# Weight splits of a fused encoder block made 2048 columns at a time, with a raw ring of two tiles and PSUM banks evacuated in pairs

## The chip, the cores and the metric

The kernel runs on one core of a Trainium2 chip. The metric is the device time of one execution in microseconds, of which less is better. A core has TensorE (PE) for matrix products, VectorE (DVE), ScalarE (ACT) and GpSimd (POOL) for elementwise work, and SyncE (SP), whose queue issues most of the DMA transfers here. PE writes its products to PSUM, eight banks of 512 float32 columns per partition; everything else works on tiles in SBUF, 128 partitions high.

## The reference

One layer of an encoder block is computed on 256 tokens of width 2048, in float32:

```
hn   = rmsnorm(x);            proj = hn @ w_in                  # 2048 x 3616
mix  = [ssd_mixer(...), pool_mixer(...)] @ w_out                # 2048 x 2048
h    = x + rmsnorm(mix)
up   = rmsnorm(h) @ w_ffn_up                                    # 2048 x 11264
ff   = (gelu(conv3(gate)) * val) @ w_ffn_down                   # 5632 x 2048
h    = h + rmsnorm(ff)
gate = sigmoid(rmsnorm(h) @ w_ple_gate)                         # 2048 x 2048
out  = h + rmsnorm(gate * (p @ w_ple))
```

Nearly all of the work is the six weight matrices. Their 51 million float32 values, some 204 MB, are read from device memory in each execution.

## The kernel before, in words

**Precision and units.** A float32 product is made from rounded operands. Each weight is split into a high part (rounded) and a low part (what the rounding left), each activation too, and PE sums three products: high by high, high by low, low by high. The weights come in units of 128 x 2048 values, 1 MB, laid out so that one DMA brings one unit. `raw` (L157) takes a tile of the ring "raw" (three tiles of 2048 columns) and has SP load a unit into it. `split` (L142) takes a pair of tiles from the rings "whi" and "wlo" (five tiles each, of 1056 columns, so half a unit), has ACT round 1024 columns into the high part (L153) and DVE subtract it from the raw values into the low part (L154). PE reads only the parts. A raw tile can be loaded again when its last split is done; a tile of parts can be written again when PE has read it for the last time. Tiles of one ring are handed out in turn, and the framework puts the waits.

**Stages.** They follow each other on PE: a first projection (`dtu`, L454, units of 1056 columns of which half come into raw tiles and half into other pages), the convolved inputs (`feature_major`, L339), then `z`, the output projection `wo`, the up projection, the down projection `dn` and the gate projection `gt`. `z`, `wo`, `dn` and `gt` go through `token_major` (L305), which works in two halves of 1024 output columns and collects products in two pairs of PSUM banks.

**The up projection** (L1007 to L1032) is the longest stage: 176 pieces of 1024 weight columns, two to a unit, four to a block of 256 output columns. Its instructions on ACT, DVE and SP run in the order in which they are written (`in_order`, L199). Five pieces are split ahead; then for each piece PE's products are issued (`feature_pairs`, L355), after the fourth piece the block's two banks are evacuated (`total`, L367: per bank an ACT copy L370 of one half and a DVE addition L371 of the other), and the piece five further on is split (`next_part`, L961), with a new unit's load at every second piece. Blocks of gate and value columns alternate by two. Between them stand the convolution, the gelu and the product of both (`gate_conv`, `gelu`, `value_out`).

**Jobs in the up projection's shadow.** A list `jobs_at` hangs further work on pieces. Thirty-seven units of `w_down` and `w_gate` are fetched (SP, L120) into pages, their four column blocks summed by DVE (`add_blocks`, L249, four additions of 512 columns), and 35 of them stored to device memory again (POOL, L244). For thirteen pairs of activation tiles, sums are made (`pair_sums`, L784: four DVE operations of 128 columns, an ACT copy, a DVE subtraction) and stored.

**Fast units.** With these sums, a unit of `dn` or `gt` needs seven block products in place of eight (`seven_products`, L255): 21 matmuls of 512 columns, where a plain unit has 24. Such a unit loads 1536 columns of weights into a raw tile (L261) and the stored sums into a page `t` (L265), and splits four times: `a` (512 columns), `b` (1024), `d` and `c` (1024 each of the sums). `dn` has 32 fast units and 12 plain ones, `gt` five fast and eleven plain, `wo` three fast, whose sums are made in place in the raw tile between the splits. `combine` (L283) then joins the seven products in PSUM. Of the second half of `gt`, the last four units are first all split and then multiplied in one pass over the output columns (tail of 4 in L321), two of them into pages kept in `spare` (L1140).

**PSUM.** The pool "pmain" has six tiles of one bank, and `main` (L83) hands them out two at a time; "pmisc" has two more.

Of the kernel before, what the change touches and what calls it, by code (L numbers as in the profile page):

```python
# [17 lines left out]
P = 128  # L18
L = 256
# [34 lines left out]
def build(nc, a, out):  # L54
# [6 lines left out]
    with tile.TileContext(nc) as tc, \  # L61
# [6 lines left out]
            tc.tile_pool(name="pmain", bufs=6, space=bass.MemoryType.PSUM) as pm, \  # L68
# [14 lines left out]
        def main(name):  # L83
            return [pm.tile([P, 512], F32, tag="main", name=f"{name}_{i}") for i in range(2)]
# [14 lines left out]
        r0 = wp.tile([P, 2048], F32, tag="raw", bufs=3, name="dtur0")  # L99
# [42 lines left out]
        def split(name, src, nel, cuts=()):  # L142

            if name in ready:
                return ready.pop(name)
            if name in spare:
                hi, lo = spare.pop(name)
            else:
                hi = wp.tile([P, 1056], F32R, tag="whi", bufs=5, name=f"{name}h")
                lo = wp.tile([P, 1056], F32R, tag="wlo", bufs=5, name=f"{name}l")  # L150
            for c0, c1 in zip((0, *cuts), (*cuts, nel)):
                s = slice(c0, c1)
                last["act"] = ins(nc.scalar.copy(hi[:, s], src[:, s]))  # L153
                last["dve"] = ins(nc.vector.tensor_sub(lo[:, s], src[:, s], hi[:, s].bitcast(F32)))  # L154
# [94 lines left out]
        def add_blocks(r):  # L249

            v = r.rearrange("p (b c) -> p b c", b=4)
            for i, j in ((1, 0), (0, 3), (3, 1), (2, 3)):
                nc.vector.tensor_add(v[:, i], v[:, i], v[:, j])  # L253

        def seven_products(name, stage, w, k0, c0, a_, acc, alt, start, stop):  # L255
# [49 lines left out]
        def token_major(name, w, c0, ks, get, acc, tail=1, fast=(), alt=None, sums=None, at=()):  # L305
# [3 lines left out]
            for u in range(nu):  # L309
# [8 lines left out]
                r = None if f"{name}{k0}_0" in ready else raw(f"{name}r{k0}", w[c0 // 1024, k0 // 2])  # L318
                for j in range(2):
                    group.append((k0 + j, *split(f"{name}{k0}_{j}", r and r[:, j * 1024:(j + 1) * 1024], 1024)))  # L320
# [18 lines left out]
        def feature_major(name, w, get, acc):  # L339

            for u in range(4):
                r = raw(f"{name}r{u}", w[u])
                for j in range(2):
                    wh, wl = split(f"{name}{u}_{j}", r[:, j * 1024:(j + 1) * 1024], 1024)
                    for kk in range(2):
                        k = 4 * u + 2 * j + kk
                        xh, xl = get(k)
                        for f in range(4):
                            s = slice(kk * 512 + f * P, kk * 512 + (f + 1) * P)
                            for q, (ww, xx) in enumerate(((wh, xh), (wh, xl), (wl, xh))):  # L350
                                mm(acc[f // 2][:, f % 2 * L:(f % 2 + 1) * L], ww[:, s], xx,
                                   k == 0 and q == 0 and f % 2 == 0, k == NK - 1 and q == 2)
                aside()

        def feature_pairs(n, part, get, acc):  # L355
# [4 lines left out]
            for kk in range(4):  # L360
                k = 4 * n + kk
                for f in range(2):
                    s = slice(kk * 256 + f * P, kk * 256 + (f + 1) * P)
                    mm(acc[f], wh[:, s], get.both(k), k == 0, False)
                    mm(acc[f][:, L:], wl[:, s], get(k)[0], False, k == NK - 1)

        def total(o, acc):  # L367

            for f in range(2):
                nc.scalar.copy(o[:, f * L:(f + 1) * L], acc[f][:, L:])  # L370
                nc.vector.tensor_add(o[:, f * L:(f + 1) * L], o[:, f * L:(f + 1) * L], acc[f][:, :L])  # L371
# [82 lines left out]
        for u in range(0, NK, 2):  # L454
            r = [wp.tile([P, 2048], F32, tag="raw", bufs=3, name=f"dtur{u}") if u else r0, page(f"dtur{u + 1}")]
# [19 lines left out]
            for j in range(2):  # L475
                k = u + j
                with tc.issue_after(front[0]), tc.issue_after(front[1]):
                    wh, wl = split(f"dtu{k}", r[j][:, :1056], 1056, ((352, 704), (704,))[k] if k < 2 else ())
# [305 lines left out]
        def pair_sums(name, s, o, a11, a21, a12, a22):  # L784


            s1, s2, s3, s4 = (s[:, i * P:(i + 1) * P] for i in range(4))
            nc.vector.tensor_sub(s1, a22, a21)
            nc.vector.tensor_sub(s3, a11, a21)
# [6 lines left out]
        def sums_in(o):  # L796
            return {f"s{i + 1}": (o[:, i * P:(i + 1) * P], o[:, 512 + i * P:512 + (i + 1) * P]) for i in range(4)}

        class Sums:
# [5 lines left out]
            def __call__(self, k):  # L805
                if k not in self.got:
                    n = len(self.got)
                    if n % 2 == 0:
# [6 lines left out]
                                            *(v[:, i * P:(i + 1) * P] for i in range(4)))  # L815
# [119 lines left out]
        def hid_sums_of(k, s, o):  # L935
            return pair_sums(f"he{k}", s, o, *(hid_part(k)[:, i * P:(i + 1) * P] for i in range(4)))
# [24 lines left out]
        def next_part():  # L961

            n = len(parts)
            if n < NPIECES:
                s, v, i = blocks[n // 4]
                name = f"u{'gv'[v]}{s}{i}"
                if n % 2 == 0:
                    slab["raw"] = raw(f"{name}r{n // 2 % 2}", w_up[v, s, i, n // 2 % 2])
                parts.append(split(f"{name}{n // 2 % 2}_{n % 2}", slab["raw"][:, n % 2 * 1024:(n % 2 + 1) * 1024], 1024))
# [37 lines left out]
        with in_order():  # L1007
            for _ in range(5):
                next_part()
            for n in range(NPIECES):  # L1010
                s, v, i = blocks[n // 4]
                if n % 4 == 0:
                    acc = main(f"{'gv'[v]}a{s}{i}")
# [9 lines left out]
                next_part()  # L1023
# [38 lines left out]
        def ple_parts():  # L1062

            r = raw("ple1r0", w_ple[1, 0])
            for j in range(2):
# [176 lines left out]
```

## Time and profile before

| what | us |
|---|---|
| timed runs, median of 3 (lowest to highest) | 1116.89 (1116.58 to 1117.33) |
| profiled execution, first to last instruction (span) | 1115.6 |
| PE busy in it | 1104.8 (99%) |
| DVE busy | 957.5 (86%) |
| ACT busy | 721.7 (65%) |
| DMA traffic | 347.29 MB, 311 GB/s over the span |

The stages in the profiled execution, by the chain of work that ended last: first projection until 53 us, convolved inputs until 142, `z` until 198, `wo` until 287, up projection from 293 to 788, down projection until 1011, gate projection to the end. "ga" and "va" are the PSUM tiles of the up projection, "dna" and "dns" those of the down projection, "gt" and "gts" of the gate. Line L90 is the helper through which every matmul goes, L120 the one for SP's loads, L153 and L154 the two halves of a split. A row of instructions has line, engine, operation, output and inputs, shapes, count, then busy time and mean ns of one, then the idle time of its engine ahead of it and what ended it. A row of waits has who waited for whom, the total, the number of times and the longest. A row of DMA issues ends with the median us from issue to landing. The lines themselves stand in the prediction.

### The profile page before, as it was taken

How to read it: one execution, taken by the hardware profiler on the slowest of the kernel's cores; microseconds unless marked ns; L12 is line 12 of the kernel's file. 1: busy time of each engine (PE TensorE's matmuls, PEld its weight loads, DVE VectorE, ACT ScalarE, POOL GpSimd, SP SyncE). 2: the span in 40 equal slices, each digit the busy share in tenths (PEclk: the TensorE clock that was granted, in tenths of full speed). 3: DMA queues.
4: the chain of work that ended last, by engine and by line, in shares of the span. 5: the costliest groups of instructions: out<-in, count | busy, mean ns of one | idle time of the engine just before them, and what ended most of it. 6: DMA issues, size and time to landing. Idle time of an engine off the chain costs nothing.

```text
span 1115.6 us, 16022 instructions
## 1 busy us (share of the span) xinstructions
PE 1104.8 (99%) x5948; PEld 951.8 (85%) x5948; DVE 957.5 (86%) x1334; ACT 721.7 (65%) x1048; POOL 68.5 (6%) x140
## 2 busy tenths in 40 slices
PE   9999999999999999999999999999999999999997
PEld 9999988888888888888888888888888888877876
DVE  6478997799868898888888888888899999989895
ACT  6847662555775564665655645657589778867673
POOL 0200000100100000000000000000000000001001
PEclk9999999999999999999999999999999999999999
DMA  9752447454599999999899999999999899996763
GB/s 362 314 194 109 164 156 284 151 189 158 199 362 401 387 378 376 359 375 369 346 377 382 354 380 366 353 391 391 361 379 382 329 343 400 418 376 229 264 237 105
DMA packets 54943, 347.29 MB, mean 311 GB/s; under 512 B 6096, under 2 KB 6992, under 8 KB 20176
## 3 DMA queue, kind: packets, MB, share of 16 engines
q1 hardware_dynamic: 44064, 289.53, 67.3%
q0 software_dynamic: 10368, 56.10, 13.4%
q8 instruction: 47, 0.77, 0.3%
q10 hardware_dynamic: 432, 0.62, 0.2%
q14 instruction: 32, 0.26, 0.1%
HBM read 297.48 MB, written 48.76 MB: 310 GB/s over the span
## 4 chain that ended last, share of the span: by engine, by line
PE 94%; DVE 2%; ACT 1%; DMA 1%; issue 1%; POOL 0%; POOLq 0%; ACTq 0%; DVEq 0%
PE ga L90 22%; PE va L90 22%; PE dna L90 12%; PE woa L90 7%; PE xbc L90 5%; PE gt L90 5%; PE z L90 4%; PE dns L90 4%; PE dtu L90 4%; PE dn0s L90 2%; PE dn1s L90 2%; DMA dtur<-w_dtu 1%; PE pw L90 1%; PE yd L90 1%; PE gts L90 1%
## 5 line engine op out<-in xcount | busy, mean ns | idle before, releaser
L90 PE MATMUL ga<-wox,ug_0h 128*128 128x512 f32 x352 | 125.5, 395 | 0.0
L90 PE MATMUL ga<-wox,ug_1h 128*128 128x512 f32 x352 | 125.1, 394 | 0.0
L90 PE MATMUL va<-wox,uv_1h 128*128 128x512 f32 x352 | 124.8, 393 | 0.0
L90 PE MATMUL va<-wox,uv_0h 128*128 128x512 f32 x352 | 124.8, 393 | 0.0
L90 PE MATMUL ga<-wox,ug_1l 128*128 128x256 f32 x352 | 99.1, 282 | 0.0
L90 PE MATMUL va<-wox,uv_1l 128*128 128x256 f32 x352 | 99.1, 281 | 0.0
L90 PE MATMUL va<-wox,uv_0l 128*128 128x256 f32 x352 | 99.1, 281 | 0.0
L90 PE MATMUL ga<-wox,ug_0l 128*128 128x256 f32 x352 | 99.0, 281 | 0.0
L253 DVE TENSOR_TENSOR dnb<-dnb 128x512 f32<-128x512 f32 x128 | 88.3, 690 | 3.1
L90 PEld LDWEIGHTS va<-wox,uv_1h 128*128 128x128 f32 x352 | 66.1, 188 | 15.0
L90 PEld LDWEIGHTS va<-wox,uv_0h 128*128 128x128 f32 x352 | 66.1, 188 | 15.0
L90 PEld LDWEIGHTS ga<-wox,ug_1h 128*128 128x128 f32 x352 | 66.1, 188 | 15.0
L90 PEld LDWEIGHTS ga<-wox,ug_0h 128*128 128x128 f32 x352 | 66.1, 188 | 14.8
L90 PEld LDWEIGHTS ga<-wox,ug_0l 128*128 128x128 f32 x352 | 66.2, 188 | 0.1
L90 PEld LDWEIGHTS ga<-wox,ug_1l 128*128 128x128 f32 x352 | 66.2, 188 | 0.0
L90 PEld LDWEIGHTS va<-wox,uv_1l 128*128 128x128 f32 x352 | 66.2, 188 | 0.0
L90 PEld LDWEIGHTS va<-wox,uv_0l 128*128 128x128 f32 x352 | 66.2, 188 | 0.0
L928 ACT CAST hs<-hid 128x512 fp32r<-128x512 f32 x44 | 27.3, 621 | 21.9 <-PE dna L90 21.6
L244 POOL DMA_DIRECT2D dns<-dnb x30 | 16.3, 542 | 309.4 <-DVE dnb L253 309.4
L929 DVE TENSOR_TENSOR hs<-hid,hs 128x512 fp32r<-128x512 f32 x44 | 30.1, 685 | 5.9 <-ACT hs L928 5.9
L792 ACT CAST he<-he 128x512 fp32r<-128x512 f32 x13 | 8.1, 621 | 36.6 <-DVE he L791 36.6
L90 PE MATMUL dna<-dn_1h,hs 128*128 128x512 f32 x96 | 30.9, 393 | 0.0
(2242 smaller groups left out, 3214.8 us busy)
## 6 DMA issues: line engine op xcount, KB each, us to landing
dnb<-w_down SPq DMA_DIRECT2D x32, 1024.0 KB, 9.9
dns<-dnb POOLq DMA_DIRECT2D x30, 1024.0 KB, 6.9
hd<-hsum POOLq DMA_DIRECT2D x24, 512.0 KB, 8.3
zr<-w_z SPq DMA_DIRECT2D x8, 1024.0 KB, 4.8
dtur<-w_dtu SPq DMA_DIRECT2D x14, 528.0 KB, 8.9
wo0r<-w_out_ SPq DMA_DIRECT2D x7, 1024.0 KB, 4.8
dn1r<-w_down SPq DMA_DIRECT2D x7, 1024.0 KB, 6.6
hsum<-he POOLq DMA_DIRECT2D x13, 512.0 KB, 7.9
```

Source lines behind the costliest of these rows:

```text
L90: last["pe"] = ins(nc.tensor.matmul(o, lhsT, rhs, start=start, stop=stop, skip_group_check=True))
L244: nc.gpsimd.dma_start(t, pg[0])
L253: nc.vector.tensor_add(v[:, i], v[:, i], v[:, j])
L792: nc.scalar.copy(o[:, :512], s[:, :512])
L928: nc.scalar.copy(t[:, :512], hid_part(k))
L929: nc.vector.tensor_sub(t[:, 512:], hid_part(k), t[:, :512].bitcast(F32))
```

## The change

Five things change together:

1. The raw ring has two tiles. The rings of parts have three tiles each of 2112 columns (`halves`). `unit` loads and splits 2048 columns with one ACT copy and one DVE subtraction. `token_major`, `feature_major` and the up projection (`next_unit`, at every second piece, three units ahead at the start) use it.
2. A fast unit splits twice: 1536 columns of weights and 2048 columns of sums. The four parts are views of the two.
3. PSUM "pmain" has three tiles of two banks. `total` evacuates both banks with one ACT copy and one DVE addition.
4. In `add_blocks` the first two additions are one of 2 x 512 columns; in `pair_sums` the first two subtractions are one of 2 x 128, and the order of the four sums in their tile changes with it.
5. In the first projection, two units of 1056 columns share a pair of parts, and the unit that took the third raw tile takes a page.

```diff
-            tc.tile_pool(name="pmain", bufs=6, space=bass.MemoryType.PSUM) as pm, \
+            tc.tile_pool(name="pmain", bufs=3, space=bass.MemoryType.PSUM) as pm, \
...
-        def split(name, src, nel, cuts=()):
-
-            if name in ready:
-                return ready.pop(name)
-            if name in spare:
-                hi, lo = spare.pop(name)
-            else:
-                hi = wp.tile([P, 1056], F32R, tag="whi", bufs=5, name=f"{name}h")
-                lo = wp.tile([P, 1056], F32R, tag="wlo", bufs=5, name=f"{name}l")
+        def halves(name):
+            return tuple(wp.tile([P, 2112], F32R, tag=f"w{q}", bufs=3, name=f"{name}{q}") for q in ("hi", "lo"))
+
+        def split(hi, lo, src, nel, cuts=()):
+
             for c0, c1 in zip((0, *cuts), (*cuts, nel)):
                 s = slice(c0, c1)
                 last["act"] = ins(nc.scalar.copy(hi[:, s], src[:, s]))
                 last["dve"] = ins(nc.vector.tensor_sub(lo[:, s], src[:, s], hi[:, s].bitcast(F32)))
-            return hi, lo
+            return hi[:, :nel], lo[:, :nel]
 
         def raw(name, src=None):
-            r = wp.tile([P, 2048], F32, tag="raw", bufs=3, name=name)
+            r = wp.tile([P, 2048], F32, tag="raw", bufs=2, name=name)
             if src is not None:
                 last["dma"] = load(r, src, True)
             return r
+
+        def unit(name, src):
+
+            if name in ready:
+                return ready.pop(name)
+            r = raw(f"{name}r", src)
+            return split(*(spare.pop(name) if name in spare else halves(name)), r, 2048)
...
             v = r.rearrange("p (b c) -> p b c", b=4)
-            for i, j in ((1, 0), (0, 3), (3, 1), (2, 3)):
+            nc.vector.tensor_add(v[:, 1::-1], v[:, 1::-1], v[:, ::3])
+            for i, j in ((3, 1), (2, 3)):
                 nc.vector.tensor_add(v[:, i], v[:, i], v[:, j])
...
-            b11 = split(f"{name}a", r[:, 512:1024], 512)
-            b2 = split(f"{name}b", r[:, 1024:], 1024)
+            bh, bl = split(*halves(f"{name}b"), r[:, 512:], 1536)
             if r is t:
                 add_blocks(r)
-            t42 = split(f"{name}d", t[:, 1024:], 1024)
-            t31 = split(f"{name}c", t[:, :1024], 1024)
+            th, tl = split(*halves(f"{name}t"), t, 2048)
+            b11, b2, t31, t42 = ((h_[:, c0:c1], l_[:, c0:c1]) for h_, l_, c0, c1 in
+                                 ((bh, bl, 0, 512), (bh, bl, 512, 1536), (th, tl, 0, 1024), (th, tl, 1024, 2048)))
...
         def total(o, acc):
 
-            for f in range(2):
-                nc.scalar.copy(o[:, f * L:(f + 1) * L], acc[f][:, L:])
-                nc.vector.tensor_add(o[:, f * L:(f + 1) * L], o[:, f * L:(f + 1) * L], acc[f][:, :L])
+            o, a_ = (v.rearrange("p (f t) -> p f t", f=2) for v in (o, acc))
+            nc.scalar.copy(o, a_[:, :, L:])
+            nc.vector.tensor_add(o, o, a_[:, :, :L])
...
-            r = [wp.tile([P, 2048], F32, tag="raw", bufs=3, name=f"dtur{u}") if u else r0, page(f"dtur{u + 1}")]
+            r = [r0 if u == 0 else page(f"dtur{u}") if u == 4 else raw(f"dtur{u}"), page(f"dtur{u + 1}")]
+            pair = halves(f"dtu{u}")
...
-            for _ in range(5):
-                next_part()
+            for _ in range(3):
+                next_unit()
...
-                next_part()
+                if n % 2:
+                    next_unit()
```

More of the change, by code (lines that the diff above doesn't have):

```diff
@@ L317, in token_major @@
                     continue
-                r = None if f"{name}{k0}_0" in ready else raw(f"{name}r{k0}", w[c0 // 1024, k0 // 2])
+                both = unit(f"{name}{k0}", w[c0 // 1024, k0 // 2])
                 for j in range(2):
-                    group.append((k0 + j, *split(f"{name}{k0}_{j}", r and r[:, j * 1024:(j + 1) * 1024], 1024)))
+                    group.append((k0 + j, *(v[:, j * 1024:(j + 1) * 1024] for v in both)))
                 if nu - tail <= u < nu - 1:
@@ L965, in next_part @@
                 s, v, i = blocks[n // 4]
[L966 to L969, printed above, removed]
+                wh, wl = unit(f"u{'gv'[v]}{s}{i}{n // 2 % 2}", w_up[v, s, i, n // 2 % 2])
+                parts.extend((wh[:, c:c + 1024], wl[:, c:c + 1024]) for c in (0, 1024))
         def gate_out(s, i, acc):
@@ L1062, in ple_parts @@
         def ple_parts():
-            r = raw("ple1r0", w_ple[1, 0])
-            for j in range(2):
-                ready[f"ple10_{j}"] = split(f"ple10_{j}", r[:, j * 1024:(j + 1) * 1024], 1024)
+            ready["ple10"] = unit("ple10", w_ple[1, 0])
         def back():
```

65 lines of the change are left out of this document (32 added, 33 removed).

## The prediction

> **What bounds the kernel now.** I read the page first: which engine is full, and which chain ends last.
>
> ```profile
> span 1115.6 us, 16022 instructions
> ...
> PE 1104.8 (99%) x5948; PEld 951.8 (85%) x5948; DVE 957.5 (86%) x1334; ACT 721.7 (65%) x1048; POOL 68.5 (6%) x140
> ...
> PE 94%; DVE 2%; ACT 1%; DMA 1%; issue 1%; POOL 0%; POOLq 0%; ACTq 0%; DVEq 0%
> ```
>
> TensorE is the bound: 10.8 us of 1115.6 are not PE time. The profiled execution agrees with the timed runs: their median, 1116.89, is 1.3 us above its span, and I carry that 1.3 along. Next the waits of PE, which show what there is to gain from shorter DVE and ACT work, and then the busy time by stage (columns: stretch, its us, PE, PEld, DVE, ACT, POOL with counts, granted clock, DMA share, GB/s).
>
> ```profile
> PE gof L90 <- ACT godg L1117: 1.9, 1, 1.9
> PE dtu L109 <- POOL ident masks.py:199: 1.4, 1, 1.4
> PE gt L90 <- DVE gt_0l L154: 0.8, 1, 0.8
> PE dtu L90 <- DVE dtu2l L154: 0.5, 1, 0.5
> PE gt L90 <- DVE gt18bl L154: 0.4, 1, 0.4
> ```
>
> ```profile
> 318.00:765.00 447.00, 447.00 (x2564) 392.37 (x2563) 387.77 (x535) 269.58 (x403) 25.85 (x48) 1.00 0.96 371
> 787.00:1012.00 225.00, 224.66 (x973) 181.57 (x972) 211.42 (x257) 175.43 (x222) 15.07 (x30) 1.00 0.95 367
> 53.00:142.00 89.00, 88.79 (x688) 85.76 (x688) 74.05 (x137) 57.78 (x97) 0.40 (x2) 1.00 0.43 154
> 142.00:198.00 56.00, 56.00 (x276) 45.72 (x275) 47.35 (x72) 28.52 (x46) 0.84 (x2) 1.00 0.55 207
> 198.00:286.00 88.00, 88.00 (x393) 71.88 (x393) 77.06 (x108) 47.98 (x69) 6.41 (x14) 1.00 0.52 189
> ```
>
> In the up projection (first row) PE never stops although the DMAs are 96% busy and DVE 87%. In the down projection (second row) the DMAs are 95% and DVE 94% busy: three resources near full, PE ahead by the depth of the staging alone. The three stages before them use the DMAs about half. So nearly nothing can be gained (DVE causes 1.7 us of PE's waits), and what decides is whether the staging still hides 371 GB/s of traffic.
>
> **The staging, before and after.** A unit is 1 MB of weights. It lands in a raw tile, ACT rounds it to a high part, DVE subtracts for the low part; DVE's last read frees the raw tile for the next load. Before: three raw tiles and five half-unit pairs of parts, 5.5 units in all. After: two raw tiles and three whole-unit pairs, 5 units. PE's period per unit is the first thing to read, from the chain in order of time (start, us): 128 matmuls are four units.
>
> ```profile
> 430.41 22.33 PE ga L90 x128
> ```
>
> ```profile
> L928 ACT CAST hs<-hid 128x512 fp32r<-128x512 f32 x44 | 27.3, 621 | 21.9 <-PE dna L90 21.6
> L153 ACT CAST ug_0h<-ug51r 128x1024 fp32r<-128x1024 f32 x2 | 2.1, 1054 | 1.8 <-PE ga L90 1.8
> L253 DVE TENSOR_TENSOR dnb<-dnb 128x512 f32<-128x512 f32 x128 | 88.3, 690 | 3.1
> L154 DVE TENSOR_TENSOR ug_1l<-ug70r,ug_1h 128x1024 fp32r<-128x1024 f32 x2 | 2.5, 1226 | 1.5 <-ACT ug_1h L153 1.5
> ```
>
> Period 22.33/4 = 5.58. ACT takes 621 ns for 512 columns and 1054 for 1024, so 433 more per 512: 1920 for 2048, 1487 for 1536. DVE: 690 and 1226, 536 more per 512: 2298 and 1762. All four are extrapolated, no row has them. A whole-unit split is ACT then DVE, 1.92 + 2.30 = **4.22 us**, where two half splits overlapped.
>
> **Term 1, the up projection.** A raw tile's turn is load time, plus any wait, plus split. Three tiles allow 3 x 5.58 = 16.7 us for a turn, two allow 11.2. The load times and one tile's life:
>
> ```profile
> ug31r<-w_up SPq DMA_DIRECT2D x2, 1024.0 KB, 7.2
> uv31r<-w_up SPq DMA_DIRECT2D x2, 1024.0 KB, 7.8
> zr<-w_z SPq DMA_DIRECT2D x8, 1024.0 KB, 4.8
> dnb<-w_down SPq DMA_DIRECT2D x32, 1024.0 KB, 9.9
> ```
>
> ```profile
> L120 SPq DMA_DIRECT2D uv40r<-w_up x2: 328/328/328, 474.5 to 481.0; - x2
> L153 ACT CAST uv_0h<-uv40r x2: 1039/1046/1054, 486.6 to 493.8; 128x1024 fp32r<-128x1024 f32 x2
> ...
> DMA to landing us min/median/max: 6.8/7.5/8.2
> ```
>
> The load issued at 474.5 has landed by 482.7, and its first split starts at 486.6: today some 4 to 5 us of slack stand between landing and use, and PE sees nothing of a late load. After the change a load of 7.75 us plus 4.22 is 11.97 against 11.17: the slack is gone, and each pair of units falls behind by 0.8 us. That is the upper end: 88 units x 0.4 = 35 us, less the lead that is used up first (a slot is freed two periods, 11.2 us, ahead of its need, the split takes 4.2, so 7): 28, or 35 if the lead is rebuilt at no point. The lower end is nothing: at 4.8 us (the z row, DMAs half used) a turn is 9.0 and fits. Which load time holds follows from the traffic. At 371 GB/s and 96%, 1 MB takes 2.7 us of the DMAs. Besides weights, a unit carries 0.4 fetch and 0.4 store of column sums: 0.85 MB, 2.3 us per 5.58. If half of what arrives during a load goes ahead of it, L = 4.8 + 0.5 x 0.41 L, 6.0 us. I take the middle of 6.0 and 7.75, **6.9**, add 0.4 for DVE's queue (four sums of 690 ns, 2.8 us, stand ahead of a split in 0.4 of the units, half served on average: 0.5), and get a turn of 11.5: 0.17 per unit, 15 us, less most of the lead, **10 us**.
>
> SP's queue matters: a load that waits for its raw tile blocks the fetch behind it, which then runs into the next load. A fetch lands after 9.9 us (the dnb row) and DVE, which works in a written order, comes to its sums three pieces (8.4 us) later; a later fetch is DVE waiting with the splits queued behind it, and PE waits for those. I keep that inside the same upper end.
>
> **Term 2, the down projection.** A fast unit is 21 matmuls, five rows of the chain from one start of nine to the next; its raw tile holds 768 KB, and the column sums come as another 1 MB.
>
> ```profile
> 818.24 5.55 PE dna L90 x24
> ...
> 834.17 2.07 PE dna L90 x9
> ...
> 839.00 2.07 PE dna L90 x9
> ```
>
> ```profile
> L120 SPq DMA_DIRECT2D dn022r<-w_down x1: 332/332/332, 827.2 to 827.2; - x1
> ...
> DMA to landing us min/median/max: 7.3/7.3/7.3
> ```
>
> Period 839.00 - 834.17 = 4.83, two make 9.66. The load takes 7.3, the split of 1536 columns 1.49 + 1.76 = 3.25: 10.55, so 0.45 us per unit over. For 32 fast units that is 14 us; with the load 1 us shorter, as in term 1, 9.55 and 0.4 of queue leave 0.15 each, 5 us. I take the middle, **9**. The 12 plain units (24 matmuls, 5.55 in the first row) just fit: 6.3 + 4.22 against 11.1. The parts' ring adds a second chain here: a unit now takes two of three slots, so the sums' split can start only when the previous unit's first tile is used up, in the changed program's order after the tenth matmul, and takes 4.22; its low part is first used at the 8th to 15th matmul of the next unit, 19 matmuls or more later. At 4.83/21 = 0.23 each that is 4.4 us: 0.2 us of cover at worst. I charge nothing; if it fails by 0.5 each, 16 us, and that stays in the range.
>
> **Term 3, the end and the seams.** The last loads of the gate projection:
>
> ```profile
> 1070.18 15.72 SPq L120 DMA_DIRECT2D gt1r<-w_gate  x4
> ```
>
> ```profile
> gt1r<-w_gate SPq DMA_DIRECT2D x6, 1024.0 KB, 4.7
> ```
>
> ```profile
> 1090.30 1.05 ACT L153 CAST gt_0h<-gt1r 128x1024 fp32r<-128x1024 f32 x1 [4.57 <-DMA gt1r<-w_gate]
> ```
>
> ```profile
> 1092.53 1.22 DVE L154 TENSOR_TENSOR gt_1l<-gt1r,gt_1h 128x1024 fp32r<-128x1024 f32 x1
> ```
>
> Four loads go out from 1070.2 to 1085.6, and the last is split as it lands. With two tiles each pair costs 4.7 + 4.2 = 8.9 us, so four units after 1070 land near 1092 and are split near 1096 instead of 1093.75 (the end of the last subtraction in the row above). **3 us**, between 0 and 9. The two PE waits on gt_0l and gt18bl above become longer by the wider subtraction, 1.07 and 0.54 us, plus their ACT part: **2**.
>
> **What costs nothing.** The merged evacuation replaces two ACT copies and two DVE additions by one each per bank pair:
>
> ```profile
> L370 ACT COPY hid<-va 128x256 f32<-128x256 f32 x44 | 15.7, 373 | 21.7 <-PE va L90 21.7
> ```
>
> The copy now waits for the second bank too, one pair of matmuls later (22.33/64 = 0.35 us), and takes about 621 for 746 ns: even, and hidden by three PSUM pairs (11 us each). A pair is freed as one where banks were freed alone; same cover; if it failed, 0.4 us per block. The merged sums save one start of DVE (154 ns, 2 x 690 - 1226) per fetch: 5 us of DVE in all, none of it on PE's path. In the xBC, z and output stages (third to fifth stage row) a turn is 4.8 + 4.2 = 9.0 against two periods of 24 matmuls, 11.1: nothing, and 4 us if a whole-unit split is late once a stage.
>
> A row against the change: in term 1, PE's waits on DVE are zero while DVE is 87% busy, so larger DVE instructions have nothing to shorten. The Trainium skill ("Perfetto Trace Analysis", Optimizing Scalar/DVE Operations) says to group when the engine is saturated, and to break instructions up when it is not but makes bubbles elsewhere. The trace so far agrees with the second half: DVE is not saturated. By the first half the sum would be at most the PE waits on DVE, -1.7 us; by the second it is a loss.
>
> **Sum.** 10 + 9 + 3 + 2 = 24; 1115.6 + 24 + 1.3 = **1141 us**, 2.2% slower.
>
> **Rivals.**
> 1. *Two tiles are enough.* If loads shorten to 6 us as soon as PE slips a little, turns fit (10.2, and 9.3 in the down projection) and only term 3 stays, 0 to 5: 1119. For it: z, output and gate loads take 4.8. Against: traffic is the same bytes in the same time. The Trainium skill ("Trainium Kernel Development and Optimization", Best Practices) asks for double buffering, not more; by that rule this rival is the outcome, and no row of this trace has a ring of two to test it.
> 2. *Load times stay.* The DMAs at 95% keep 7.75 and 7.3: 28 + 14 + 5, with the parts' ring failing by 0.5 per fast unit 16 more: 47 to 63, some 1172.
> 3. *Faster.* DVE frees 0.15 us per unit and the seams' DVE chains (1.7 us of PE's waits, 0.3 on ACT) vanish: -2.5 at most, 1114.4. It decides only if both rings keep ahead of PE and the seams' splits are ordered before the critical additions. Against: those very waits are for one subtraction, which gets longer.
>
> **Chances.** Forecast (1124 to 1158) 0.58; rival 1 0.17; rival 2 0.18; rival 3 0.07. A measurement tells about 0.2%, 2.2 us, from no change. Rival 3 gives faster 0.06 and same 0.01; rival 1 is half within, half slower: same 0.10, slower 0.84 in all. The range leaves out rival 3 and the far end of rival 2: 1118 to 1170.
>
> **What would show it.** Right: PE waits on ug/uv and dn low and high parts appear inside the up and down projections, ACT's casts wait for DMA w_up where today they wait for PE; DMA share falls under 0.95; load medians fall to 6 or 7. Wrong: PE busy stays 447 of 447 in the up projection (rival 1), or loads stay near 7.7 with PE gaps at every second unit (rival 2), or the PE gaps stand at the halves' turns alone. If PE waits in the down projection name the sums' split while raw tiles have landed, the parts' ring, not the raw ring, was mis-sized.

## The result, and the profile after

The changed kernel takes 1196.8 us, the median of runs from 1187.1 to 1201.9; the kernel before took 1117.1 beside it. The ratio is 1.070, 95% interval 1.066 to 1.075: **7% slower**, where 2.2% was forecast and the range ended at 1170. The page of the changed kernel:

```profile
span 1199.8 us, 15136 instructions
...
PE 1137.4 (95%) x5948; PEld 962.6 (80%) x5948; DVE 937.0 (78%) x997; ACT 684.9 (57%) x778; POOL 76.2 (6%) x140
...
PEclk9999999999799999999999999999999999999988
...
PE 8%; DVE 4%; DMA 4%; ACT 3%; issue 1%; POOL 0%; SPq 0%; POOLq 0%; ACTq 0%; DVEq 0%
```

PE does the same 5948 matmuls and has 62 us in which it isn't busy, where it had 10.8. Its busy time for them has grown too, from 1104.8 to 1137.4 us. DVE and ACT do less than before. The chain that ends last is followed back for the last fifth of the span only, and in that fifth DVE, DMAs and ACT take more than PE, which had 94% of the chain before. PE's waits, which were five short ones, are now (who waited for whom, us, times, longest):

```profile
PE gof L94 <- ACT godg L1121: 7.5, 1, 7.5
PE woxt L398 <- DVE wox L198: 4.0, 1, 4.0
PE woxt L398 <- DVE h L859: 3.8, 1, 3.8
PE dna L94 <- ACT dn122thi L153: 3.3, 1, 3.3
PE woa L94 <- ACT wo10thi L153: 2.8, 1, 2.8
PE ga L94 <- DVE ug610lo L154: 2.7, 1, 2.7
PE gts L94 <- DVE gt18blo L154: 2.3, 1, 2.3
```

Splits of the up and down projections are among them, as forecast. But the longest stand at the seams between stages (woxt is the transposing of the output stage's result, gof the very end), and there the prediction had charged almost nothing. The stretches of the up projection, the down projection, the gate projection and the output stage, columns as in the prediction:

```profile
340.00:790.00 450.00, 444.72 (x2511) 385.29 (x2510) 355.36 (x346) 241.96 (x270) 23.99 (x45) 1.00 0.91 350
829.00:1080.00 251.00, 233.10 (x969) 179.95 (x968) 210.37 (x173) 164.08 (x142) 15.52 (x27) 0.99 0.88 338
1088.00:1186.00 98.00, 93.62 (x421) 76.52 (x419) 74.01 (x85) 55.16 (x67) 5.79 (x13) 0.95 0.52 195
203.00:299.00 96.00, 90.29 (x395) 72.67 (x395) 73.90 (x81) 44.82 (x50) 8.75 (x12) 0.98 0.42 156
```

The DMA share has fallen from 0.96 and 0.95 to 0.91 and 0.88, as one expects where loads wait for a free tile. In the first row the count tells more than the busy time: 2511 matmuls at 32 per unit are 78.5 units in 450 us, 5.73 us each, where the period had been 5.58. Not all of that is waiting, as a run below shows. The granted clock under 1.00 was not there before.

To know where the 84 us between the two profiled executions (1115.6 and 1199.8) lie, I take each stage from its first matmul to its last, by the trace. The rows between stand for experiments that follow; each is the difference to the row above it, so that they sum to the whole. In order they are the kernel before with banks in pairs, then the changed kernel with three raw tiles, first with splits cut at 1024 columns and then with whole ones.

| profiled execution | until `wo` | `wo` | end of `wo` to `dn` | `dn` | after `dn` | span |
|---|---|---|---|---|---|---|
| before | 198.2 | 88.1 | 501.3 | 223.0 | 105.0 | 1115.6 |
| banks in pairs | +0.6 | +0.3 | +5.3 | +1.6 | +3.5 | +11.3 |
| three whole pairs of parts, splits cut at 1024, merges | +0.2 | -0.6 | +2.9 | -1.5 | +3.9 | +4.8 |
| splits not cut | +2.2 | +3.5 | -3.1 | +3.1 | +5.2 | +11.0 |
| two raw tiles for three | +1.9 | +4.3 | +24.2 | +24.3 | +2.4 | +57.0 |
| after | 203.1 | 95.6 | 530.6 | 250.5 | 120.0 | 1199.8 |

Single executions of the slower kernels differ by some us (the changed one by 15), so the small entries are rough; the medians give +11.5, 0.0, +15.6 and +52.6 for the four steps. The third column also holds a difference of pace between these executions that is no waiting; it is taken apart at the run with three raw tiles and cut splits.

### The profile page after: what moved, and what is told of

Same layout as the page of the kernel before. It is cut to its first block, busy times and chain, and to the rows that moved or that the text cites. A ratio compares the mean times of both kernels' runs of the same rounds, so it can differ in the third digit from the quotient of the medians.

```text
span 1199.8 us, 15136 instructions
## 1 busy us (share of the span) xinstructions
PE 1137.4 (95%) x5948; PEld 962.6 (80%) x5948; DVE 937.0 (78%) x997; ACT 684.9 (57%) x778; POOL 76.2 (6%) x140
## 3 DMA queue, kind: packets, MB, share of 16 engines
q0 software_dynamic: 10368, 56.10, 11.4%
## 5 line engine op out<-in xcount | busy, mean ns | idle before, releaser
L261 DVE TENSOR_TENSOR dnb<-dnb 128x512 f32<-128x512 f32 x64 | 44.3, 692 | 2.1
L259 DVE TENSOR_TENSOR dnb<-dnb 128x1024 f32<-128x1024 f32 x32 | 39.0, 1219 | 0.0
L996 ACT ACTIVATE fc<-gr,vt 128x256 f32<-128x256 f32 x44 | 26.1, 593 | 12.3 <-DVE gr L989 12.3
L998 ACT ACTIVATE gr<-gr,vt 128x256 f32<-128x256 f32 x44 | 22.5, 511 | 1.4
L997 ACT ACTIVATE ft<-gr,vt 128x256 f32<-128x256 f32 x44 | 21.8, 495 | 0.0
L446 DVE SCALAR_TENSOR_TENSOR cv<-xr,vt,cv 128x254 f32<-128x254 f32 (+1 forms) x48 | 19.5, 479 | 0.3 <-ACT cv L440 0.3
L999 DVE TENSOR_TENSOR fc<-fc,ft 128x510 f32<-128x510 f32 x22 | 15.1, 688 | 4.4 <-ACT ft L997 4.0
L1000 DVE TENSOR_TENSOR fc<-fc,gr 128x510 f32<-128x510 f32 x22 | 15.2, 691 | 2.3
L989 DVE TENSOR_TENSOR gr<-gr,rfb 128x512 f32<-128x512 f32 x22 | 15.2, 692 | 0.8
L1012 DVE TENSOR_TENSOR hid<-hid,fc 128x512 f32<-128x512 f32 x22 | 15.2, 692 | 0.8
```

The source lines that it names most:

```text
L259: nc.vector.tensor_add(v[:, 1::-1], v[:, 1::-1], v[:, ::3])
L446: nc.vector.scalar_tensor_tensor(o[:, lo:hi], i[:, lo + d:hi + d], vec(wcol + j * wstep + f), o[:, lo:hi], op0=ALU.mult, op1=ALU.add)
L996: nc.scalar.activation(c[:, f], v[:, f], AF.Identity, bias=vec(V_FCB + 4 * s + 2 * i + f), scale=vec(w + NF))
L997: nc.scalar.activation(l[:, f], v[:, f], AF.Copy, scale=vec(w))
L998: nc.scalar.activation(v[:, f], v[:, f], AF.Copy, scale=vec(w + 2 * NF))
```

## Experiments

**The ring alone, the ring undone, the splits cut, the merges alone.** First the two suspects, each way round. Of every edit only the lines that matter are shown. *Two raw tiles in the kernel before* (and, as in the change, one unit of the first projection in a page):

```diff
-            r = wp.tile([P, 2048], F32, tag="raw", bufs=3, name=name)
+            r = wp.tile([P, 2048], F32, tag="raw", bufs=2, name=name)
```

> The kernel before with one number changed: two raw tiles in place of three (and, as in the change, one unit of the first projection in a page). The half-unit splits and the five pairs of parts stay. Theory R (the raw ring is the cause): a tile's turn is a load of 6 to 8 us and two half splits, some 3.5 us, so most of the loss comes back: 1160 to 1195 us, PE waiting in the down projection and at the seams. Rival W (the wide splits and their ring of three pairs are the cause): 1117 to 1130.

Measured: 1217.1 us, ratio 1.087 (1.081 to 1.092). W falls. R holds in kind, but the loss is larger than it said, and larger than that of the whole change; it comes back below.

*A third raw tile in the changed kernel.* To make room for it, this kernel leaves out the three gain vectors: one value is broadcast in their place, and three loads of 1 MB go, which the changed kernel issues at 172, 813 and 1086 us.

```diff
-            r = wp.tile([P, 2048], F32, tag="raw", bufs=2, name=name)
+            r = wp.tile([P, 2048], F32, tag="raw", bufs=3, name=name)
```

> The changed kernel with a third raw tile; to make room for it, the three gain vectors are left out of the computation (one value is broadcast in their place, the multiplications stay, three loads of 1 MB go). Theory R: nearly all of the loss of 80 us goes, 1115 to 1135 us. Rival W: the ring of three pairs still paces, 1165 to 1200. If each is half of it: 1140 to 1160.

Measured: 1144.2 us, 1.026 (1.021 to 1.032). By the numbers this is the third case: the ring has two thirds of it, 53 of the 80 us, and something else 27. What the three loads cost is within the 53 and isn't separated; none of them is issued in the up projection before its last 17 us. The up projection's middle is whole again, with all of its traffic:

```profile
340.00:790.00 450.00, 450.00 (x2598) 393.54 (x2597) 377.56 (x369) 253.99 (x284) 26.87 (x50) 1.00 0.97 370
```

*Splits cut in two, rings as in the change* (a fast unit's two splits are cut likewise):

```diff
-            return split(*(spare.pop(name) if name in spare else halves(name)), r, 2048)
+            return split(*(spare.pop(name) if name in spare else halves(name)), r, 2048, (1024,))
```

> The changed kernel with each split cut again at 1024 columns (512 and 1024 for the weights of a fast unit), into the same wide pairs; rings as in the change. Theory R: the turn of a raw tile gets 0.7 us shorter (a rounding overlaps a subtraction) and nothing else: 1175 to 1195 us. Rival W in the form that a long instruction delays what is queued behind it: 1130 to 1165. Rival W in the form that three whole pairs are too few: no change, 1190 to 1202.

Measured: 1165.3 us, 1.044 (1.041 to 1.048), 31 us better than the change: at the upper end of what W gave for long instructions in the way, and 10 below what R gave for the turn alone. A cut helps both ways, so this run by itself doesn't separate them; that three whole pairs are too few, however they are filled, is excluded as the cause of the loss.

*Bank pairs, merged evacuation and merged sums in the kernel before* (parts 3 and 4 of the change as they stand in its diff, from this line on):

```diff
-            tc.tile_pool(name="pmain", bufs=6, space=bass.MemoryType.PSUM) as pm, \
+            tc.tile_pool(name="pmain", bufs=3, space=bass.MemoryType.PSUM) as pm, \
```

> The kernel before with parts 3 and 4 of the change alone: PSUM handed out in pairs of banks, both evacuated at once, the first additions of the sums merged. All theories price these at nothing: 1114 to 1119 us. If the pairing of banks carries part of the loss, over 1122.

Measured: 1127.5 us, 1.009 (1.008 to 1.011). The price of nothing, on which all theories agreed, was wrong by 10 us.

**What the merges cost, what stays with three tiles, and what the traffic does.** *The merged sums alone:*

```diff
-            for i, j in ((1, 0), (0, 3), (3, 1), (2, 3)):
+            nc.vector.tensor_add(v[:, 1::-1], v[:, 1::-1], v[:, ::3])
+            for i, j in ((3, 1), (2, 3)):
```

> The kernel before with part 4 alone (first additions of the sums merged). Theory P (the 10.6 us of parts 3 and 4 together come from banks handed out in pairs): 1116 to 1118 us. Rival (the merged sums shift DVE's order at the seams): over 1122.

Measured: 1117.4 us, 1.0001 (0.9992 to 1.0010). Nothing, as forecast.

*Banks in pairs, nothing merged* (three tiles of two banks; `both_banks` allocates one):

```diff
         def main(name):
-            return [pm.tile([P, 512], F32, tag="main", name=f"{name}_{i}") for i in range(2)]
+            o = both_banks(name)
+            return [o[:, :512], o[:, 512:]]
```

> The kernel before with PSUM handed out in pairs and nothing merged: each bank is still evacuated by instructions of its own. Theory P (a reader of one bank of a pair waits until the other is written too, and a pair comes free as one): 1124 to 1129 us, lost at the seams and in the last tail. Rival (the merged evacuation in the up projection costs it): 1116 to 1118.

Measured: 1128.6 us, 1.010 (1.009 to 1.011). Theory P holds: the pairs alone cost it, and not the merged evacuation. The trace of the last stage shows how. These are ACT's tanh instructions on the last banks in the kernel before (start, us, instruction, idle time and releaser):

```profile
1100.95 0.69 ACT L1154 ACTIVATE gth<-gt,rh 128x512 f32<-128x512 f32 x1 [2.34 <-PE gt L90]
...
1104.17 0.46 ACT L1154 ACTIVATE gth<-gt,rh 128x256 f32<-128x256 f32 x1
...
1106.71 0.47 ACT L1154 ACTIVATE gth<-gts,rh 128x256 f32<-128x256 f32 x1 [1.09 <-PE gts L90]
```

and with banks in pairs:

```profile
1114.61 1.05 ACT L1158 ACTIVATE gth<-gt,rh 128x512 f32<-128x512 f32 x2 [3.28 <-PE gt L94]
...
1117.28 0.45 ACT L1158 ACTIVATE gth<-gts,rh 128x256 f32<-128x256 f32 x1
```

Before, the first bank is read 3.2 us ahead of the second, while PE still writes there. In the pair the two instructions (x2) run one right after the other, when PE is done with the second bank and has gone on to `gts` (from 1114.4). From there the chain to the last output is longer: PE's wait for godg at the end goes from 1.9 to 4.3 us. The largest entry of the pairs' row in the table, 5.3 us behind the end of `wo`, was not followed instruction by instruction. That the reader waits because the two banks are one tile to the framework is inferred from this.

*Three raw tiles and cut splits* (both kinds of unit, the gain vectors left out as before):

```diff
-            bh, bl = split(*halves(f"{name}b"), r[:, 512:], 1536)
+            bh, bl = split(*halves(f"{name}b"), r[:, 512:], 1536, (512,))
```

> The changed kernel with three raw tiles (the gain vectors left out of the computation to make room, as in the run with three tiles and wide splits) and with each split cut again at 1024 columns. Theory G (what stays with three raw tiles, 27 us, is 10.6 us of bank pairs and 17 us of wide splits at the seams): 1125 to 1132 us. Rival (the ring of three whole pairs costs the 17 us, however the split is cut): 1140 to 1146.

Measured: 1128.6 us, 1.010 (1.007 to 1.013), the same as bank pairs alone. So G holds by the medians: three whole pairs of parts cost nothing, and uncut splits cost 15.6 us.

The table's third column, where uncut splits seem to save 3.1 us, needs one more look. In the middle of the up projection PE is busy all the time in this kernel as in the one with uncut splits, whose row stands above, and yet gets through 49 matmuls fewer:

```profile
340.00:790.00 450.00, 450.00 (x2549) 390.57 (x2548) 374.71 (x442) 254.23 (x354) 26.08 (x49) 1.00 0.97 365
```

Where nothing waits, one matmul of 512 columns and one of 256 take 348.9 ns together, from start to start, in the kernel before; 349.1 with banks in pairs, 353.2 here, 346.7 with uncut splits and three tiles, 352.3 in the changed kernel. Over the stage's 1408 such couples this is +0.3, +5.8, -9.2 and +7.9 us of the column's four steps. Without it the steps are +5.0, -2.9, +6.1 and +16.3: uncut splits do cost at the seam, where the first up matmul comes 13.0 us after the last of `wo` and not 7.1, and the ring costs 16 there and not 24. Why the pace differs no run here shows. The timed executions of single kernels spread by as much (1123.6 to 1133.5 with cut splits, 1142.0 to 1153.9 with uncut ones), so it may belong to the execution and not to the kernel.

*The sums of columns left out of the up projection's shadow* (nothing is stored there either, and DVE's additions go with the traffic):

```diff
-        dn_fast, gt_fast = ((2, 3, 4, 5, 7, 8, 9, 10, 11, 12, 13, 14, 15, 16, 17, 18, 19), (2, 3, 4, 5, 7, 8, 9, 11, 12, 13, 14, 15, 16, 18, 19)), ((4, 5, 6), (1, 2))
+        dn_fast, gt_fast = ((), ()), ((), (1, 2))
```

> The changed kernel with the sums of columns left out of the up projection's shadow (no fetches, additions and stores beyond two units), so that the down projection and the first half of the gate have plain units only; the output is the same. Only the up projection is compared, 517.9 us with two raw tiles and 494.5 before. Theory T (two raw tiles fail because a load takes over 6 us beside that traffic; alone it takes 4.8 us, and 4.8 + 4.2 us fit into two periods of 5.58): 494 to 503 us, the seam's loss at its start included, loads of 4.8 to 5.2 us. Rival (the pacing of the splits fails, whatever the load takes): 510 to 520 us. The whole time says little, 1180 to 1230, since 37 units take 24 matmuls in place of 21.

Measured: up projection 499.7 us, as theory T had it, in one execution. Some 8 of the 18 us against the changed kernel are pace again (346.7 ns a couple), but in its middle PE doesn't wait at all and does as many matmuls as with three tiles. The middle, and the life of one unit there (load issued, landing, rounding, subtraction):

```profile
340.00:790.00 450.00, 450.00 (x2599) 396.82 (x2598) 275.57 (x211) 245.93 (x270) 1.33 (x2) 1.00 0.56 197
```

```profile
L124 SPq DMA_DIRECT2D uv710r<-w_up x1: 327/327/327, 650.2 to 650.2; - x1
L153 ACT CAST uv710hi<-uv710r x1: 1921/1921/1921, 657.1 to 657.1; 128x2048 fp32r<-128x2048 f32 x1
...
DMA to landing us min/median/max: 4.7/4.7/4.7
```

Two raw tiles and uncut splits do hide a traffic of 197 GB/s: the load takes 4.7 us and lies ready 2.2 us before ACT takes it. That DVE has less to do isn't the reason: by the table of turns below, the shorter load takes 1.6 us off a turn of 11.8 and the shorter split 0.4, and two periods are 11.2. This unit of the changed kernel, at 350 GB/s, was late:

```profile
L124 SPq DMA_DIRECT2D ug810r<-w_up x1: 328/328/328, 687.6 to 687.6; - x1
L153 ACT CAST ug810hi<-ug810r x1: 1919/1919/1919, 695.8 to 695.8; 128x2048 fp32r<-128x2048 f32 x1
L154 DVE TENSOR_TENSOR ug810lo<-ug810r,ug810hi x1: 2283/2283/2283, 700.0 to 700.0; 128x2048 fp32r<-128x2048 f32 x1
...
DMA to landing us min/median/max: 7.5/7.5/7.5
```

Its load took 7.5, the split started 0.7 after landing, and the subtraction stood 2.3 us in DVE's order: the turn was 14.7 us, against the 11.2 that two periods give. The whole time, 1172.6 in one run, is 24 us under the changed kernel's: with two tiles the seven-product units, 21 matmuls for 24, and their column sums cost more than they save.

**Why the ring alone is worse than the whole change.** *Two raw tiles, and six half-unit pairs in place of five:*

```diff
-                hi = wp.tile([P, 1056], F32R, tag="whi", bufs=5, name=f"{name}h")
+                hi = wp.tile([P, 1056], F32R, tag="whi", bufs=6, name=f"{name}h")
```

> The kernel before with two raw tiles, and six pairs of half-unit parts in place of five (three units, as many as the change has). The ring of two alone gave 1217 us, 20 more than the whole change. Theory Q (the half-unit order holds a raw tile longer: its second half is split one piece of 2.8 us after its first, so a turn is a load of 6.6 us + 2.8 + 1 + 1.2, over 11.2): no help from depth, 1205 to 1220 us, up projection 545 to 562. Rival D (five halves were too few): 1160 to 1185, up projection 500 to 520.

Measured: 1212.5 us, 1.084 (1.080 to 1.088), up projection 550.6. Depth doesn't help; D falls. *The same, with both halves of a unit split at every second piece:*

```diff
-            for _ in range(5):
+            for _ in range(6):
                 next_part()
...
-                next_part()
+                for _ in range(n % 2 * 2):
+                    next_part()
```

> As the run with two raw tiles and six half-unit pairs, but both halves of a unit are split one after the other at every second piece, as the change does. Theory Q: a raw tile is held 2 us shorter in the up projection, whose time falls to 500 to 520 us, the whole to 1165 to 1185. Rival D: like the run with six pairs, within 8 us.

Measured: 1173.9 us, 1.051 (1.049 to 1.053), up projection 516.8. Theory Q holds. Two units share each of these rows (first and last start), the subtractions of the first and second halves, for six pairs:

```profile
L154 DVE TENSOR_TENSOR uv_0l<-uv70r,uv_0h x2: 1218/1222/1226, 672.9 to 678.9; 128x1024 fp32r<-128x1024 f32 x2
L154 DVE TENSOR_TENSOR uv_1l<-uv70r,uv_1h x2: 1218/1219/1220, 674.0 to 682.9; 128x1024 fp32r<-128x1024 f32 x2
```

and with both halves at once:

```profile
L154 DVE TENSOR_TENSOR uv_0l<-uv70r,uv_0h x2: 1219/1222/1226, 652.6 to 658.6; 128x1024 fp32r<-128x1024 f32 x2
L154 DVE TENSOR_TENSOR uv_1l<-uv70r,uv_1h x2: 1218/1218/1218, 653.7 to 659.7; 128x1024 fp32r<-128x1024 f32 x2
```

The second unit's halves stand 4.0 us apart in the one, 1.1 in the other, and so long the raw tile is kept. Thus splitting the whole unit at once, in part 1 of the change, gives back in the up projection some 34 us of what its ring of two takes (550.6 to 516.8 here; from two tiles and five halves to the whole change, in which other things differ too, 559.6 to 517.9).

One sum covers these runs. For each load of the up projection but the first four I took the time from its issue to the end of the last subtraction that reads the tile, its *turn*, and the mean distance between issues from the seventh load on, the *period* (from the fifth on it is 5.92 in the second row and 5.64 in the fourth):

| kernel | load | landed until split | split | turn | turn / tiles | period |
|---|---|---|---|---|---|---|
| before (3 tiles) | 8.0 | 3.1 | 5.5 | 16.6 | 5.5 | 5.56 |
| after (2) | 6.6 | 0.6 | 4.7 | 11.8 | 5.9 | 5.83 |
| after, cut (2) | 6.9 | 0.4 | 4.0 | 11.4 | 5.7 | 5.71 |
| after, little traffic (2) | 5.0 | 2.0 | 4.25 | 11.25 | 5.6 | 5.54 |
| before with 2 tiles | 6.7 | 0.4 | 5.5 | 12.6 | 6.3 | 6.29 |
| same, 6 pairs, both halves at once | 6.9 | 0.5 | 4.1 | 11.5 | 5.8 | 5.79 |

Each next load goes out 0.03 us after its tile is free, so turn over tiles must be the period, and is in every row, to 0.1 us. This alone doesn't tell what sets the pace; the time between landing and split does. Where PE sets the pace (first and fourth row) the turn holds slack, 3.1 and 2.0 us between landing and split; where the ring does, that slack is 0.4 to 0.6.

**The seam.** DVE's order at the seam from `wo` to the up projection in the changed kernel:

```profile
305.04 2.29 DVE L154 TENSOR_TENSOR ug001lo<-ug001r,ug001hi 128x2048 fp32r<-128x2048 f32 x1 [2.66 <-ACT ug001hi L153]
307.25 0.69 DVE L852 TENSOR_TENSOR wom<-woa,gmix 128x512 f32<-128x512 f32 x1
307.85 0.74 DVE L859 SCALAR_TENSOR_TENSOR h<-wom,wo0r,h 128x512 f32<-128x512 f32 x1
```

The next stage's split waits 2.7 us for its load, runs 2.3, and `wom` and `h`, for which PE waits, stand behind it. In the next run these splits stand behind the stage's own last steps (here the second and third unit):

```diff
+            with tc.issue_after(held[0]), tc.issue_after(held[1]):
+                next_unit()
+                next_unit()
```

> The changed kernel with the up projection's second and third unit split after the output stage's last squares and additions, and its fourth after the last piece of the new panel (order on ACT and DVE alone). Theory S (at this seam whole-unit splits that wait for a load stand ahead of the stage's own last steps, and PE waits for those): from the last matmul of the output stage to the first of the down projection 530.5 us falls by 6 to 14; the whole 1183 to 1192. Rival (the seam is late because of the load itself or of the bank pairs): 527 to 535 us there.

Measured: 1200.0 us, 1.074 (1.073 to 1.076), and 533.3 us from the end of `wo` to `dn` in place of 530.6. The seam itself became shorter (first up matmul 8.9 us after the end of `wo`, not 12.6; PE's longest wait for `wox` 1.9, not 4.0), but PE then waited more inside the up projection: without those at the transposes, its pauses of over 0.3 us there (from one start to the next, less a matmul's own time) sum to some 16.6 us, not 8.5. So S falls as a cost of its own. What fits this, though no run tests it apart: while the ring sets the pace, a stall at the seam is time in which the ring gets ahead, and without it the same time is waited for later. That such splits cost where the ring isn't the bound is what the pair of runs with three tiles shows (uncut 1144.2, cut 1128.6).

**The clock.** The trace of the changed kernel has ten segments at half the granted clock (nine of 3.4 us, one of 10.2) and a last one in the idle tail, 49.5 us in all, in which matmuls took some 17 us longer than at full clock. In the next run the kernel before gets seven short pauses:

```diff
             total(hd, acc)
+            if (s, i) in short:
+                mm(misc("pause")[:, :P], ident, hd[:, 512 - P:], True, True)
             nc.vector.tensor_mul(hd, hd, slab[s][1][:, i * 512:(i + 1) * 512])
+            if (s, i) in long:
+                mm(misc("pause")[:, :P], ident, hd[:, 512 - P:], True, True)
```

> The kernel before with seven extra matmuls of 128 columns in the up projection, each of which makes PE wait for the evacuation of the block just finished: three wait for its addition (an idle time of 1.2 to 1.7 us), four for the product with the gelu after it (2 to 2.6 us). Theory K (an idle time of PE over some 1.8 us is followed by 3.4 us at half the granted clock): four half-clock segments behind the long pauses, none behind the short ones; about 13 us for the idle times and 4 x 1.7 for the clock, 1137 us. Rival (the clock falls for other reasons, such as a whole slice of little work): no segment, 1130 us.

Measured: 1142.3 us, 1.023 (1.021 to 1.025): 5 us over theory K, of which 3 are the pauses, 16.4 us in sum (those for the addition 2.31, 0.9 and 2.32, those for the product 1.64, 3.63, 1.65 and 3.92). Three were followed by half clock, not four (2.32, 3.63 and 3.92), and 2.31 wasn't, so length alone doesn't decide. Rows of windows of 3.41 us, on the grid on which the clock changes: a pause of 2.32 us and the window behind it, one of 1.64 and the window behind it, and one of 2.31 that falls into two windows, with the one behind them:

```profile
556.58:559.99 3.41, 1.09 (x8) 0.72 (x7) 2.80 (x6) 1.67 (x3) 0.53 (x1) 1.00 0.89 375
559.99:563.40 3.41, 3.41 (x13) 2.93 (x12) 1.67 (x2) 0.00 (x0) 0.00 (x0) 0.50 0.99 315
604.36:607.77 3.41, 1.77 (x11) 1.33 (x9) 2.84 (x5) 1.83 (x4) 0.00 (x0) 1.00 0.94 358
607.77:611.18 3.41, 3.41 (x21) 3.01 (x22) 0.98 (x1) 0.29 (x1) 0.00 (x0) 1.00 1.01 420
...
461.00:464.41 3.41, 2.38 (x14) 1.83 (x12) 3.31 (x6) 1.92 (x4) 0.28 (x1) 1.00 1.01 425
464.41:467.82 3.41, 2.13 (x13) 1.90 (x14) 2.83 (x5) 0.32 (x1) 0.26 (x1) 1.00 0.97 339
467.82:471.23 3.41, 3.41 (x21) 2.97 (x21) 1.45 (x2) 1.05 (x1) 0.00 (x0) 1.00 0.97 372
```

After a window in which PE was busy for 1.09 of 3.41 us, the next runs at 0.50, 13 matmuls instead of 21. After 1.77, or after 2.38 and 2.13, it runs at 1.00. Theory K is right in kind and wrong in its rule: what counts here is PE's share of a window, not the length of the pause. The last section has all traces for this.

## Why the prediction was wrong

Right by its own steps: PE as the bound with nearly nothing to gain, hence the sign; a whole-unit split at 1.92 + 2.30 us (1919 and 2283 ns in the rows of `ug810r`; 1482 and 1757 ns for 1536 columns); loads between 6.0 and 7.75 (mean 6.6 in the up projection); ACT's roundings waiting for loads and DMA share falling; the merged sums and merged evacuation at nothing; the parts' ring of three at nothing. The mechanism of terms 1 and 2, a raw tile's turn against two periods, is the cause of 53 of the 80 us by the medians. Two readings were loose: the load issued at 474.5 took 6.8 us (8.2 was the one issued at 481.0), and 7.75 us stands in no row shown; the mean of the stage's loads was 8.0. What failed are the sizes, and some prices of nothing:

1. **Term 1, the up projection: 10 forecast, 24 measured.** The turn came out at 11.8, not 11.5: the load was 0.3 shorter, but waits for busy engines inside the turn were 0.6 before and 0.4 within the split, 1.0 in place of 0.4 us. The queue of the engines is the part that was mis-sized. Of the 24 us some 8 are the slower pace, which the sum didn't have; 16 are waiting. "Less most of the lead" fits them: PE's own period in this trace is 16 x 352.3 ns = 5.64 us, (11.8 - 11.27)/2 x 88 = 23 us is the loss by the turn, and 7 remain for the lead, as the prediction had it. This is worked out from the turns; no run shows the lead by itself.
2. **Term 2, the down projection: 9 forecast, 24 for the ring, 27.5 in all.** I took the middle between a load of 7.3 and one a us shorter, and added DVE's queue to the shorter only. This is the unit that the prediction used:

```profile
L124 SPq DMA_DIRECT2D dn022r<-w_down x1: 328/328/328, 880.2 to 880.2; - x1
L153 ACT CAST dn022bhi<-dn022r x1: 1482/1482/1482, 888.5 to 888.5; 128x1536 fp32r<-128x1536 f32 x1
L154 DVE TENSOR_TENSOR dn022blo<-dn022r,dn022bhi x1: 1757/1757/1757, 890.0 to 890.0; 128x1536 fp32r<-128x1536 f32 x1
...
DMA to landing us min/median/max: 8.2/8.2/8.2
```

   Issued at 880.2, free at 891.8: a turn of 11.6 where 9.95 to 10.55 was assumed. Over all 44 weight loads of the stage the mean turn is 11.2 (load 6.6, wait 0.75, split 3.8), 5.6 per unit. The issues stand 5.59 apart from the third load on, 5.10 before, 22 us over 44 units. The load lies within what was assumed, 6.3 to 7.3. Mis-sized were the waits for busy engines: 0.75 us ahead of the split and 0.3 inside it (3.8, where 32 splits of 3.25 and 12 of 4.22 have a mean of 3.5).
3. **"A pair is freed as one where banks were freed alone; same cover": 11.5 us, forecast nothing.** Cover was checked inside the up projection, where three pairs suffice, and not at the seams and the end; in the last stage the trace shows a first bank's evacuation on the chain. And what a pair delays isn't only the freeing but the first read.
4. **"In the xBC, z and output stages: nothing, and 4 us if late", and term 3's 3 + 2: 12 and 15 us.** Up to the end of `wo` 12.4 us are lost, after `dn` 15.0. The ring has 6.2 and 2.4 of them, uncut splits 5.7 and 5.2, pairs 0.9 and 3.5; 3.9 after `dn` stand in the step to three whole pairs and were not followed. The turn of 9.0 us against 11.1 was a sum for a steady stage; at its ends an uncut split can stand ahead of the stage's own last steps, as the seam behind `wo` shows, and a row of busy times doesn't.
5. **The clock wasn't in the sum at all.** The kernel before showed 1.00 in all its stages, so no row had a price for it; it adds to pauses that leave PE busy for less than some half of a window, about 17 us of the 84 in this trace. These are part of the steps above, not a further step.

Rival 2 (loads stay, 1172) was nearest in its terms for the two projections, 28 and 14, but by luck: its condition failed, since the loads did shrink from 8.0 to 6.6 us. Rival 1's rule holds with its condition: two tiles are enough at loads of 5.0 us. The Trainium skill ("Trainium Kernel Development and Optimization", Best Practices) asks for double buffering. By these runs, two buffers hide a traffic of 197 GB/s here; at 350 GB/s two don't, and three hide 370. Nothing between was run. What the skill says of instruction size ("Perfetto Trace Analysis", Optimizing Scalar/DVE Operations) is borne out in its second half: DVE was not saturated (78% busy), and cutting the splits again took 31 us off with two raw tiles, in part by a shorter turn (11.4 for 11.8), and 15.6 with three.

## What to carry to other kernels

For a ring of buffers, add up the whole turn: load at its loaded duration, wait for the engine, and every instruction until the last read. Turn over number of buffers is the period, and what is over the bound's period is lost at each unit, once the slack at the start is used up. Before giving a stage's whole difference to waiting, count the bound engine's instructions where it is busy all the time: its own pace can differ between two traces. Price steps at the ends of stages by the chain there, not by a stage's mean load, and before joining two buffers into one tile look for a reader that needs only the first.

## What the hardware showed

The granted clock goes by PE's busy share in windows of 3.41 us on a fixed grid. In the 14 traces of this study, the idle tails left out, all 43 windows at full clock with PE busy for under 46% were followed by half clock, and none of those with over 53%. Between the two both occur (8 of 22). A window at half clock in which PE was busy for up to 83% was followed by another, and one with 90% or more was not. The Trainium skill ("TensorE: Matmul & The Clock Gate", "What's actually happening") has the free-running window of 3413 ns and half the clock after an idle window, and gives as the rule for kernels no idle time over some 3.4 us ("HAM oscillation — how this bites in real kernels"). The window and the half agree; the rule is too lax, since 2.32 us inside one window were enough.
